# A hybrid decoder trunk: attention heads taken in pairs, with one output projection for both

## The chip, the cores and the metric

The kernel runs on one core of a Trainium2 chip. The metric is the device time of one execution in microseconds (us); lower is better. The core's engines have queues of their own and run beside each other: TensorE (PE, with its weight loads shown as PEld), VectorE (DVE), ScalarE (ACT), GpSimd (POOL) and SyncE (SP), which issues the DMAs. Matmuls write into PSUM, which has eight banks of 128 x 512 float32; DVE and ACT read them from there.

## The reference, cut to what matters

Two layers act on x of 1024 tokens by 1024 channels. Layer 0 mixes the tokens by a gated recurrence (HGRN2), layer 1 by latent attention (MLA) with 8 heads; behind each mixer stands a convolutional gated MLP. The change is in the attention:

```python
q = (_rmsnorm(c_q, q_a_norm) @ w_q_up).reshape(B, S, MLA_HEADS, MLA_QK_HEAD)
kv = (_rmsnorm(c_kv, kv_a_norm) @ w_kv_up).reshape(B, S, MLA_HEADS, MLA_NOPE + MLA_V_HEAD)
...
q = _rope_tail(_rmsnorm(q, q_norm), cos, sin)
k = _rope_tail(_rmsnorm(k, k_norm), cos, sin)
o = _causal_block_attention(q, k, v)
return o.reshape(B, S, MLA_HEADS * MLA_V_HEAD) @ w_out
...
x = x + y
h = _rmsnorm(x, norm_ffn[layer])
x = x + _conv_ffn(h, ffn_w_up[layer], ffn_conv_w[layer], ffn_conv_b[layer], ffn_w_down[layer])
```

The last product runs over all heads at once; the kernel sums it head by head.

## The kernel before, in words

The residual stream stays on the chip, transposed: two tiles `xt[0]` and `xt[1]`, one for each half of 512 tokens, each with 8 blocks of 128 channels. Float32 operands are split into a high and a low part (`split`, L124: ACT casts the high part at L126, DVE or POOL subtracts at L129), and each product is three matmuls: high by high, high by low, low by high (`acc3`, L142, matmuls at L145 to L147). Weights come by a DMA on SP's queue into one of two raw buffers (`fetch_w`, L86) and are split into one of three slots of the weight pool (`load_w`, L131); the output weight of a head has a slot of its own (tag "wo").

`mla` (L531) runs over the heads. For a head, `kproj` (L617) and `knorm` (L629) make its keys, `qproj` (L642) the queries of one half, `vproj` (L668) the values of two heads. `attend(hd, b, ...)` (L686) does two blocks of 128 queries, b from 0 to 3: scores at L701 into one of three banks, maxima on DVE (L706), exponentials on ACT (L716), scaling on POOL (L721), transposes at L730 with their split, the product with the values at L742 to L744 into a single bank, and a split of the result into the head's output tile, which holds one half. b = 0 and 1 fill the first half, 2 and 3 the second. Larger b have more keys and cost more.

`wout` (L748) is the output projection of one head and one half: for each of 8 channel blocks three matmuls of 512 columns into one of two banks ("mm", which all projections share), and `add_x` (L298) adds the bank to `xt` on DVE (L299). So head by head the residual is added to. The loop at L780 takes, for a head: attend 0, the second half's `wout` of the head before (`late`), the next head's `kproj`, attend 1, the next head's first `qproj`, attend 2, `wout` of the first half, the next head's `knorm`, attend 3, the next head's second `qproj`. Output tiles have two buffers. Keys alternate between the buffers "hh0" and "hh1", values lie in "hl1", the query latents in "hl0".

Behind the last head's attend 3 stands `first_half(1)` (L274): the norm of `xt[0]` for the MLP that follows (`normalize`, L261: sum of squares over the channels by `token_scale`, L200; scaling in place on DVE at L266; `xt` is also written to memory), and the split of its two halves of channels, LO and HI, into "hh0" and "hl0" (`operand`, L269). Then come the last `wout`, and in the MLP `second_half` (L278), for tokens 512 to 1023, and `open_strips` (L250): products of eight weight strips with the first half's two operands (L247), which need nothing of the second half. `hgrn` (L302) uses `first_half(0)` in the same way.

The program's order isn't written out by hand: a planner orders each engine's instructions ahead of time, by the order of the code and by when it expects them to be ready, and a later instruction may go ahead of an earlier one that isn't ready. On the chip each engine follows the order that is so fixed.

Of the kernel before, what the change touches and what calls it, by code (L numbers as in the profile page):

```python
# [10 lines left out]
F32R = mybir.dt.float32r  # L11
# [8 lines left out]
P = 128  # L20
D = 1024
S = 1024
HF = 512
KD = D // P
HEADS = 8
# [33 lines left out]
def trunk_kernel(ctx: ExitStack, tc: tile.TileContext, x, pos, par, gout, cst, msk, w_hin, w_hout,  # L59
# [6 lines left out]
    hpool = ctx.enter_context(tc.tile_pool(name="hpool", bufs=1))  # L66
# [4 lines left out]
    def ps_mm():  # L71
        return psg.tile([P, HF], F32, tag="mm", name="ps_mm")
# [8 lines left out]
    xt = [t.rearrange("p (k n) -> p k n", k=KD) for t in xflat]  # L81
# [49 lines left out]
    def load_w(src, tag="w", wp=None, bufs=3, eng=pool):  # L131
        lo_eng = dve if first else eng
        raw = first.pop(0) if first else fetch_w(src)
        hi = (wp or wpool).tile([P, 1024], F32R, tag=tag + "hi", name="whi", bufs=bufs)
        lo = (wp or wpool).tile([P, 1024], F32R, tag=tag + "lo", name="wlo", bufs=bufs)
        split(raw, hi, lo, lo_eng=lo_eng)
        return hi, lo

    def v3(ap, a):
        return ap.rearrange("p (a b) -> p a b", a=a)  # L140

    def acc3(ps, steps):  # L142
        n = len(steps)
        for i, (lh, ll, rh, rl) in enumerate(steps):
            pe.matmul(ps, lhsT=lh, rhs=rh, start=(i == 0), stop=False)  # L145
            pe.matmul(ps, lhsT=lh, rhs=rl, start=False, stop=False)  # L146
            pe.matmul(ps, lhsT=ll, rhs=rh, start=False, stop=(i == n - 1))  # L147
# [74 lines left out]
    def norm_x(hf, which, layer, spread=True, lo_eng=pool):  # L222
# [9 lines left out]
            return hh, hl, y, v  # L232
        return hh, hl, spread_scale(hf, y, lo_eng), y

    KH = KD // 2
    LO, HI = slice(0, KH), slice(KH, KD)
    OPENED = tuple(range(1, 17, 2))
# [5 lines left out]
    def product(p, a, b, first=True):  # L243
        for k in range(KH):
            ks = slice(k * P, (k + 1) * P)
# [23 lines left out]
    def operand(src, wp, tag):  # L269
        t = wp.tile([P, 2, KH, HF], F32R, tag=tag, name="bop", bufs=1)  # L270
        split(src, t[:, 0], t[:, 1], lo_eng=dve)
        return t

    def first_half(layer):  # L274
        normalize(0, layer)
        return [operand(xt[0][:, LO, :], hpool, "hh0"), operand(xt[0][:, HI, :], hpool, "hl0")]

    def second_half(layer, ep):  # L278
        normalize(1, layer)
# [251 lines left out]
    def mla(h):  # L531
        with ExitStack() as st:
            tp = st.enter_context(tc.tile_pool(name="m_t", bufs=2))
# [69 lines left out]

            wts = {}

            def weights(pr):
                wts["q", pr] = [v3(t, 2).rearrange("p k (h c) -> p k h c", h=2) for t in load_w(w_qup[pr])]
                wts["kv", pr] = [v3(t, 2).rearrange("p k (h c) -> p k h c", h=2) for t in load_w(w_kvup[pr])]

            def lora(w, c, hd, c0, hf):  # L610
                p = ps_mm()
# [5 lines left out]
            def kproj(hd):  # L617
                kgs, sqs = [], []
                for hf in range(2):
                    p = lora(wts["kv", hd // 2], ckv, hd, 0, hf)  # L620
                    sq = tpool.tile([P, HF], F32, tag="sq", name="ksq")
                    act.activation(out=sq, in_=p, func=AF.Square)
                    kg = tpool.tile([P, HF], F32, tag=f"rb{hf}", name="kg", bufs=1)
                    act.activation(out=kg, in_=p, func=AF.Identity, scale=pcol("kn", 0))
                    kgs.append(kg)
                    sqs.append([sq])
                return kgs, token_rstd(sqs, QK, krs.rearrange("p a b -> p (a b)"), tag="wo")

            def knorm(hd, kgs, y):  # L629
                kk = hpool.tile([P, 4, S], F32R, tag=f"hh{hd % 2}", name="kk")  # L630
                for hf in range(2):
                    sl = slice(hf * HF, (hf + 1) * HF)
                    rb = bcast(y[:, 4 * hf:4 * hf + 4], tag="wo")
                    kg = kgs[hf]
                    dve.tensor_tensor(out=kg, in0=kg, in1=rb, op=ALU.mult)
                    split(kg, kk[:, 0, sl], kk[:, 1, sl], lo_eng=dve)
                    kt = tpool.tile([P, HF], F32, tag="acc", name="kt", bufs=1)
                    dve.tensor_tensor(out=kt, in0=krot[:, hf, :], in1=rb, op=ALU.mult)
                    split(kt, kk[:, 2, sl], kk[:, 3, sl])
                return kk  # L640

            def qproj(hd, hf):  # L642
                qq = tp.tile([P, 3, HF], F32R, tag="q", name="qq")
                pn = lora(wts["q", hd // 2], cq, hd, 0, hf)
                pt = lora(wts["q", hd // 2], cq, hd, P, hf)
                sq = tpool.tile([P, HF], F32, tag="sq", name="qsq")
                act.activation(out=sq, in_=pn, func=AF.Square)
                sq2 = tpool.tile([P, HF], F32, tag="sq", name="qsq2")
                act.activation(out=sq2[0:64, :], in_=pt[0:64, :], func=AF.Square)
                pool.tensor_tensor(out=sq[0:64, :], in0=sq[0:64, :], in1=sq2[0:64, :], op=ALU.add)  # L650
                y = token_rstd([[sq]], QK, vq[:, hf, :], tag="wo")
                rq = tp.tile([P, 4], F32, tag="rq", name="rq")
                dve.tensor_scalar(out=rq, in0=y, scalar1=float(QK ** -0.5), scalar2=None, op0=ALU.mult)
                act.activation(out=qq[:, 0, :], in_=pn, func=AF.Identity, scale=pcol("qn", 0))
                dve.scalar_tensor_tensor(out=qq[:, 1, :], in0=pn, scalar=pcol("qn", 0),
                                         in1=qq[:, 0, :].bitcast(F32), op0=ALU.mult, op1=ALU.subtract)
                qt = tp.tile([P, 2, HF], F32, tag="qt", name="qt", bufs=1)
                for i in range(2):
                    rows = slice(64 * i, 64 * i + 64)
                    dve.scalar_tensor_tensor(out=qt[0:64, i, :], in0=pt[rows, :], scalar=pcol("qt", 0)[rows],  # L660
                                             in1=rope_t[rows, hf, :], op0=ALU.mult, op1=ALU.mult)
                rot = qt[0:64, 0, :]
                pool.tensor_tensor(out=rot, in0=rot, in1=qt[0:64, 1, :], op=ALU.add)
                act.copy(out=qq[0:64, 2, :], in_=rot)
                pool.tensor_tensor(out=qq[64:P, 2, :], in0=rot, in1=qq[0:64, 2, :].bitcast(F32), op=ALU.subtract)
                return qq, rq
# [78 lines left out]
                sl = slice((b % 2) * 2 * P, (b % 2 + 1) * 2 * P)  # L745
                split(po, oh[:, sl], ol[:, sl], lo_eng=dve)

            def wout(hf, wo, o):  # L748
                for d in range(KD):
                    p = ps_mm()  # L750
                    acc3(p, [(wo[0][:, d * P:(d + 1) * P], wo[1][:, d * P:(d + 1) * P], o[0], o[1])])
                    add_x(hf, d, p)

            def otile():
                return (tp.tile([P, HF], F32R, tag="oh", name="oh"), tp.tile([P, HF], F32R, tag="ol", name="ol"))

            wk = [load_w(w_min[2]), load_w(w_min[3])]
            wr = load_w(w_min[4])
# [6 lines left out]
            cq = clora(wq, cq_tile, "qa", 0, vq[:, 0, :], ps_s)  # L765
            h[1] = h[1]()
            clora(wk, ckv, "kva", 1, vc[:, 1, :])
            weights(0)
            rootc(0)
            ropek(wr, 1)  # L770
            rootc(1)
            kp = kproj(0)
            clora(wq, cq, "qa", 1, vq[:, 1, :], ps_s)
            kk = knorm(0, *kp)
            dve.tensor_scalar(out=vq, in0=vq, scalar1=EPS, scalar2=None, op0=ALU.mult)
            q0 = qproj(0, 0)
            vv = vproj(0)
            q1 = qproj(0, 1)
            late = None
            for hd in range(HEADS):  # L780
                more = hd + 1 < HEADS
                if more and hd % 2 == 1:
                    weights((hd + 1) // 2)
                o0 = otile()
                attend(hd, 0, kk, vv, *q0, *o0)
                if late:
                    wout(*late)
                wo = load_w(w_mout[hd], "wo", tp, 1)
                if more:
                    kp = kproj(hd + 1)  # L790
                attend(hd, 1, kk, vv, *q0, *o0)
                if more:
                    q0 = qproj(hd + 1, 0)
                o1 = otile()
                if not more:
                    wout(0, wo, o0)
                attend(hd, 2, kk, vv, *q1, *o1)
                if more:
                    wout(0, wo, o0)
                if more:  # L800
                    kk2 = knorm(hd + 1, *kp)
                attend(hd, 3, kk, vv, *q1, *o1)
                if not more:
                    h2 = first_half(1)
                late = (1, wo, o1)
                if more:
                    kk = kk2
                    q1 = qproj(hd + 1, 1)
                    if hd % 2 == 1:
                        vv = vproj((hd + 1) // 2)  # L810
            wout(*late)
            return h2

# [158 lines left out]
    h = [norm_x(0, "mix", 0, lo_eng=dve)]  # L972
    h = hgrn(0, h)
    h = ffn(0, h)
    h = mla(h)
# [77 lines left out]
```

## Time and profile before

| | us |
|---|---|
| median of 3 runs | 2605.51 |
| lowest, highest | 2604.63, 2606.7 |
| the profiled execution's own time | 2608.18 |
| its span, first to last instruction | 2606.4 |
| matmuls busy (share of the span) | 2474.9 (95%) |
| weight loads busy | 2043.3 (78%) |
| VectorE busy | 1795.3 (69%) |
| ScalarE busy | 1026.1 (39%) |
| GpSimd busy | 504.7 (19%) |

The profile shows one execution. Busy time is the union of an engine's instructions; matmuls are pipelined and overlap, so a busy PE isn't a PE at its peak. The granted clock of TensorE is 1.00 at full speed (2.4 GHz) and 0.5 at half. The attention's heads run from about 1440 to 1908 us of the span, the MLP of layer 1 follows. A row of the timeline has the start, the duration, the engine, the line, what is written and read, the count of merged instructions, and in brackets the engine's idle time before it and what ended it.

### The profile page before, as it was taken

The page shows a single profiled execution, that of the slowest core. Times are in us where ns is not written, and L with a number is a line of the kernel's source. Part 1 is how long each engine was busy: PE and PEld are TensorE (multiplying, and loading weights), DVE is VectorE, ACT ScalarE, POOL GpSimd, SP SyncE. Part 2 cuts the span into 40 slices and gives each one's busy share as a digit, 9 for nine tenths or more (in the row PEclk, how much of TensorE's full clock was granted, in tenths as well). Part 3 has the DMA queues.
Part 4 walks back from the last instruction along what each step waited for, and adds up shares of the span by engine and source line. Part 5 has one row for each costly group of instructions (what it writes and reads, how often), then busy time and mean ns, then how long its engine had stood idle before and what let it go on. Part 6 is the DMA issues. An engine that isn't in the chain of part 4 may idle for free.

```text
span 2606.4 us, 35442 instructions
## 1 busy us (share of the span) xinstructions
PE 2474.9 (95%) x13732; PEld 2043.3 (78%) x13732; DVE 1795.3 (69%) x3218; ACT 1026.1 (39%) x1697; POOL 504.7 (19%) x489
## 2 busy tenths in 40 slices
PE   7999999998889999999999999999879999999999
PEld 6888888887667778888888777777757777888887
DVE  7455565667778888774545887877878888875333
ACT  4322222232444444433433444444434444443322
POOL 4343333543000000000013444443400000000000
PEclk9999999999999999999999899999989999999999
DMA  3011100211323232264431000000033332226443
GB/s 145 34 41 41 33 33 25 74 59 56 117 97 117 105 107 90 95 226 154 137 115 57 9 17 17 17 25 9 33 123 123 110 109 101 97 88 223 153 169 119
DMA packets 67561, 228.21 MB, mean 88 GB/s; under 512 B 7616, under 2 KB 8000, under 8 KB 66240
## 3 DMA queue, kind: packets, MB, share of 16 engines
q1 hardware_dynamic: 67392, 225.94, 24.5%
q8 instruction: 108, 1.77, 0.3%
q14 instruction: 61, 0.50, 0.1%
HBM read 181.87 MB, written 44.04 MB: 87 GB/s over the span
## 4 chain that ended last, share of the span: by engine, by line
PE 77%; DVE 16%; ACT 3%; issue 2%; DMA 1%; POOL 0%; ACTq 0%; DVEq 0%; SPq 0%; POOLq 0%
PE ps_mm L247 18%; PE ps_up L247 8%; PE ps_up L946 7%; PE ps_mm L145 6%; PE ps_mm L147 6%; PE ps_mm L146 6%; PE ps_mm L946 5%; PE ps_wo L946 4%; PE ps_wo L247 3%; PE sc L388 2%; PE ps_misc L946 2%; DVE x L299 2%; PE sp L701 2%; PE ps_wo L145 1%; DMA wraw<-in_w_up_dram 1%
## 5 line engine op out<-in xcount | busy, mean ns | idle before, releaser
L126 ACT CAST whi<-wraw 128x1024 fp32r<-128x1024 f32 (+1 forms) x312 | 304.9, 991 | 564.1 <-PE ps_misc L946 240.9
L247 PE MATMUL ps_mm<-bop,whi 128*128 128x512 f32 x1536 | 485.3, 398 | 40.2 <-ACT bop L126 15.8
L129 DVE TENSOR_TENSOR wlo<-wraw,whi 128x1024 fp32r<-128x1024 f32 (+1 forms) x266 | 299.5, 1139 | 286.0 <-ACT whi L126 282.6
L247 PEld LDWEIGHTS ps_mm<-bop,whi 128*128 128x128 f32 x1536 | 290.3, 191 | 115.2 <-ACT bop L126 16.3
L247 PE MATMUL ps_mm<-bop,wlo 128*128 128x512 f32 x768 | 299.7, 395 | 0.9 <-DVE wlo L129 0.9
L866 DVE SCALAR_TENSOR_TENSOR x<-x,prm,x 128x1023 f32<-128x1023 f32 (+1 forms) x176 | 223.6, 1280 | 50.5 <-ACT x L863 49.5
L247 PE MATMUL ps_up<-bop,whi 128*128 128x512 f32 x704 | 221.6, 395 | 0.4 <-ACT whi L126 0.4
L247 PEld LDWEIGHTS ps_mm<-bop,wlo 128*128 128x128 f32 x768 | 146.2, 190 | 33.6 <-DVE wlo L129 1.4
L946 PE MATMUL ps_up<-ring,whi 128*128 128x512 f32 x528 | 159.8, 389 | 0.0
L247 PEld LDWEIGHTS ps_up<-bop,whi 128*128 128x128 f32 x704 | 132.0, 188 | 32.5 <-ACT whi L126 2.0
L129 POOL TENSOR_TENSOR wlo<-wraw,whi 128x1024 fp32r<-128x1024 f32 x46 | 113.2, 2463 | 219.3 <-ACT whi L126 219.3
L145 PE MATMUL ps_mm<-vgh,hh 128*128 128x256 f32 x512 | 145.1, 284 | 5.4 <-DVE q L355 5.4
L147 PE MATMUL ps_mm<-vgh,hl 128*128 128x256 f32 x512 | 145.0, 283 | 0.0
L146 PE MATMUL ps_mm<-vgl,hh 128*128 128x256 f32 x512 | 143.7, 281 | 0.0
L247 PE MATMUL ps_up<-bop,wlo 128*128 128x512 f32 x352 | 138.5, 394 | 0.0
L399 DVE TENSOR_TENSOR Q<-Q,tot 128x256 f32<-128x256 f32 x96 | 63.0, 656 | 103.7 <-PE sc L388 79.8
L863 ACT ACTIVATE x<-x,prm 128x1024 f32<-128x1024 f32 x88 | 109.5, 1244 | 62.0 <-DVE x L890 38.3
L701 PE MATMUL sp<-kk,qq 128*128 128x384 f32 (+4 forms) x480 | 112.1, 363 | 16.6 <-ACT pp L716 13.5
L849 DVE TENSOR_TENSOR wraw<-wraw 128x512 f32<-128x512 f32 x176 | 121.0, 688 | 2.1
L145 PE MATMUL ps_mm<-hh,whi 128*128 128x512 f32 x288 | 115.6, 402 | 2.5 <-DVE g L375 1.6
L401 POOL TENSOR_TENSOR K<-K,tot 128x256 f32<-128x256 f32 x96 | 78.4, 816 | 192.8 <-PE sc L388 124.1
L946 PEld LDWEIGHTS ps_up<-ring,whi 128*128 128x128 f32 x528 | 99.1, 188 | 20.6
(302 smaller groups left out, 5689.6 us busy)
## 6 DMA issues: line engine op xcount, KB each, us to landing
wraw<-in_w_up_dram SPq DMA_DIRECT2D x104, 512.0 KB, 3.7
wraw<-in_w_down_dram SPq DMA_DIRECT2D x88, 512.0 KB, 3.5
act_spill<-x SPq DMA_DIRECT2D x44, 512.0 KB, 2.6
araw<-act_spill SPq DMA_DIRECT2D x88, 256.0 KB, 3.6
wraw<-in_w_hin_dram SPq DMA_DIRECT2D x38, 512.0 KB, 3.5
x_spill<-x SPq DMA_DIRECT2D x4, 2048.0 KB, 6.7
open_spill<-part SPq DMA_DIRECT2D x32, 256.0 KB, 2.3
x<-open_spill SPq DMA_DIRECT2D x16, 512.0 KB, 3.2
```

The costliest lines, as they stand in the source:

```text
L126: act.copy(out=hi, in_=src)
L129: lo_eng.tensor_tensor(out=lo, in0=src, in1=hi.bitcast(F32), op=ALU.subtract)
L145: pe.matmul(ps, lhsT=lh, rhs=rh, start=(i == 0), stop=False)
L146: pe.matmul(ps, lhsT=lh, rhs=rl, start=False, stop=False)
L147: pe.matmul(ps, lhsT=ll, rhs=rh, start=False, stop=(i == n - 1))
L247: pe.matmul(p, lhsT=a[l][:, ks], rhs=b[:, r, k, :], start=first and k == 0 and n == 0, stop=k == KH - 1 and n == 2, skip_group_check=not f ...
L401: pool.tensor_tensor(out=Kv[:, :, 0, :], in0=Kv[:, :, 0, :], in1=tv[:, :, 1:2].broadcast_to([P, nb, m]), op=ALU.mult)
L701: pe.matmul(sp[:, 0:n], lhsT=qq[:, a, qs], rhs=kk[:, c, cl], start=(i == 0), stop=last)
L849: dve.tensor_tensor(out=o, in0=p, in1=q, op=op)
L863: act.activation(out=y, in_=u, func=AF.Identity, scale=cw(2, ff), bias=pcol("cb", layer * 44 + ff))
L866: dve.scalar_tensor_tensor(out=y[:, i:S], in0=u[:, 0:S - i], scalar=cw(2 - i, ff), in1=y[:, i:S], op0=ALU.mult, op1=ALU.add)
L946: pe.matmul(acc[d], lhsT=w[l][:, d * P:(d + 1) * P], rhs=a[:, r], start=j == 0 and n == 0, stop=j == NFF - 1 and n == 2)
```

## The change

Heads are taken in pairs a, b. The order is: attend 0 of a, `kproj` of b, the late `wout` of the pair before, attend 1 of a, `knorm` and first `qproj` of b, attends 0 and 1 of b with a's second `qproj` between them, `wout` of the first half for both heads, attends 2 and 3 of a with b's second `qproj` between, attends 2 and 3 of b with the next pair's keys and first queries between. `wout` takes both heads into the same bank, six matmuls for each of the 8 blocks, and adds once. The second output weight comes into one of the three slots of the weight pool. Query and key-value weights are loaded apart, at different places. In the last pair `first_half(1)` stands behind attend 3 of a. In `first_half` LO goes into "hl0" and HI into "hh0". The output tiles keep two buffers, now written out.

```diff
@@ -232,6 +232,7 @@
             return hh, hl, y, v
         return hh, hl, spread_scale(hf, y, lo_eng), y
 
+    OB = 2
     KH = KD // 2
     LO, HI = slice(0, KH), slice(KH, KD)
     OPENED = tuple(range(1, 17, 2))
@@ -273,7 +274,7 @@
 
     def first_half(layer):
         normalize(0, layer)
-        return [operand(xt[0][:, LO, :], hpool, "hh0"), operand(xt[0][:, HI, :], hpool, "hl0")]
+        return [operand(xt[0][:, LO, :], hpool, "hl0"), operand(xt[0][:, HI, :], hpool, "hh0")]
 
     def second_half(layer, ep):
         normalize(1, layer)
@@ -603,9 +604,9 @@
 
             wts = {}
 
-            def weights(pr):
-                wts["q", pr] = [v3(t, 2).rearrange("p k (h c) -> p k h c", h=2) for t in load_w(w_qup[pr])]
-                wts["kv", pr] = [v3(t, 2).rearrange("p k (h c) -> p k h c", h=2) for t in load_w(w_kvup[pr])]
+            def weights(kind, pr):
+                w = (w_qup if kind == "q" else w_kvup)[pr]
+                wts[kind, pr] = [v3(t, 2).rearrange("p k (h c) -> p k h c", h=2) for t in load_w(w)]
 
             def lora(w, c, hd, c0, hf):
                 p = ps_mm()
@@ -745,14 +746,16 @@
                 sl = slice((b % 2) * 2 * P, (b % 2 + 1) * 2 * P)
                 split(po, oh[:, sl], ol[:, sl], lo_eng=dve)
 
-            def wout(hf, wo, o):
+            def wout(hf, pair):
                 for d in range(KD):
+                    ds = slice(d * P, (d + 1) * P)
                     p = ps_mm()
-                    acc3(p, [(wo[0][:, d * P:(d + 1) * P], wo[1][:, d * P:(d + 1) * P], o[0], o[1])])
+                    acc3(p, [(wo[0][:, ds], wo[1][:, ds], o[0], o[1]) for wo, o in pair])
                     add_x(hf, d, p)
 
             def otile():
-                return (tp.tile([P, HF], F32R, tag="oh", name="oh"), tp.tile([P, HF], F32R, tag="ol", name="ol"))
+                return (tp.tile([P, HF], F32R, tag="oh", name="oh", bufs=OB),
+                        tp.tile([P, HF], F32R, tag="ol", name="ol", bufs=OB))
 
             wk = [load_w(w_min[2]), load_w(w_min[3])]
             wr = load_w(w_min[4])
@@ -765,7 +768,8 @@
             cq = clora(wq, cq_tile, "qa", 0, vq[:, 0, :], ps_s)
             h[1] = h[1]()
             clora(wk, ckv, "kva", 1, vc[:, 1, :])
-            weights(0)
+            weights("q", 0)
+            weights("kv", 0)
             rootc(0)
             ropek(wr, 1)
             rootc(1)
@@ -775,39 +779,44 @@
             dve.tensor_scalar(out=vq, in0=vq, scalar1=EPS, scalar2=None, op0=ALU.mult)
             q0 = qproj(0, 0)
             vv = vproj(0)
-            q1 = qproj(0, 1)
             late = None
-            for hd in range(HEADS):
-                more = hd + 1 < HEADS
-                if more and hd % 2 == 1:
-                    weights((hd + 1) // 2)
-                o0 = otile()
-                attend(hd, 0, kk, vv, *q0, *o0)
+            for a in range(0, HEADS, 2):
+                b, pr = a + 1, a // 2
+                more = b + 1 < HEADS
+                oa, ob = otile(), otile()
+                attend(a, 0, kk, vv, *q0, *oa)
+                kp = kproj(b)
                 if late:
                     wout(*late)
-                wo = load_w(w_mout[hd], "wo", tp, 1)
+                wos = [load_w(w_mout[a], "wo", tp, 1), load_w(w_mout[b])]
+                attend(a, 1, kk, vv, *q0, *oa)
+                kb = knorm(b, *kp)
+                q0 = qproj(b, 0)
                 if more:
-                    kp = kproj(hd + 1)
-                attend(hd, 1, kk, vv, *q0, *o0)
+                    weights("kv", pr + 1)
+                attend(b, 0, kb, vv, *q0, *ob)
+                q1 = qproj(a, 1)
+                attend(b, 1, kb, vv, *q0, *ob)
+                wout(0, list(zip(wos, (oa, ob))))
+                oa, ob = otile(), otile()
+                attend(a, 2, kk, vv, *q1, *oa)
+                q0 = qproj(b, 1)
                 if more:
-                    q0 = qproj(hd + 1, 0)
-                o1 = otile()
-                if not more:
-                    wout(0, wo, o0)
-                attend(hd, 2, kk, vv, *q1, *o1)
+                    weights("q", pr + 1)
+                attend(a, 3, kk, vv, *q1, *oa)
                 if more:
-                    wout(0, wo, o0)
+                    kp = kproj(b + 1)
+                else:
+                    h2 = first_half(1)
+                attend(b, 2, kb, vv, *q0, *ob)
                 if more:
-                    kk2 = knorm(hd + 1, *kp)
-                attend(hd, 3, kk, vv, *q1, *o1)
-                if not more:
-                    h2 = first_half(1)
-                late = (1, wo, o1)
+                    kk = knorm(b + 1, *kp)
+                    q1 = qproj(b + 1, 0)
+                attend(b, 3, kb, vv, *q0, *ob)
+                late = (1, list(zip(wos, (oa, ob))))
                 if more:
-                    kk = kk2
-                    q1 = qproj(hd + 1, 1)
-                    if hd % 2 == 1:
-                        vv = vproj((hd + 1) // 2)
+                    vv = vproj(pr + 1)
+                    q0 = q1
             wout(*late)
             return h2
```

## Rows read from the trace of the kernel before

**Rows 1.** The page, part 1: busy us, share of the span, instructions.

```profile
PE 2474.9 (95%) x13732; PEld 2043.3 (78%) x13732; DVE 1795.3 (69%) x3218; ACT 1026.1 (39%) x1697; POOL 504.7 (19%) x489
```

**Rows 2.** Busy time by stretch: start:end, length, then each engine's busy us.

```profile
core 0: us, PE busy (x) PEld busy (x) DVE busy (x) ACT busy (x) POOL busy (x), PEclk, DMA share, GB/s
...
1552.00:1669.00 117.00, 106.43 (x620) 86.55 (x619) 96.16 (x253) 54.55 (x120) 49.32 (x57) 1.00 0.06 19
...
1876.00:1892.00 16.00, 11.77 (x66) 9.64 (x66) 14.03 (x30) 10.58 (x24) 7.45 (x8) 1.00 0.20 81
1892.00:1908.50 16.50, 14.55 (x69) 10.83 (x69) 10.28 (x27) 4.41 (x8) 0.57 (x3) 0.90 0.20 82
1908.50:1924.00 15.50, 2.40 (x5) 1.09 (x6) 14.19 (x18) 7.24 (x8) 4.44 (x3) 0.58 0.32 135
```

**Rows 3.** Timeline of PE in an output projection, around 1666 us.

```profile
1665.99 0.50 PE L145 MATMUL ps_mm<-oh,whi 128*128 128x512 f32 x1 [0.43 <-DVE x L299]
...
1666.56 0.39 PE L147 MATMUL ps_mm<-oh,wlo 128*128 128x512 f32 x1
1666.79 0.62 PE L701 MATMUL sp<-kk,qq 128*128 128x256 f32 x4
```

**Rows 4.** Waits, 1440 to 1925 us: total us, times, longest us.

```profile
PEld ps_mm L145 <- DVE x L299: 22.4, 40, 1.3
PEld sp L701 <- ACT pp L716: 20.0, 23, 1.8
...
PE ps_mm L145 <- DVE x L299: 7.5, 14, 0.9
```

**Rows 5.** Groups by line, 1440 to 1925 us: count, busy us, mean ns, idle before.

```profile
L299 DVE TENSOR_TENSOR x<-x,ps_mm 128x512 f32<-128x512 f32 x128 | 86.0, 680 | 4.5 <-PE ps_mm L147 3.6
...
L129 POOL TENSOR_TENSOR wlo<-wraw,whi 128x1024 fp32r<-128x1024 f32 x12 | 28.9, 2407 | 45.3 <-ACT whi L126 45.3
...
L126 ACT CAST whi<-wraw 128x1024 fp32r<-128x1024 f32 x15 | 15.8, 1051 | 36.7 <-PE ps_mm L146 32.0 <-DMA wraw<-in_w_qup_dram 2.5 <-DMA wraw<-in_w_up_dram 2.0
```

**Rows 6.** The chain that ended last, 1440 to 1925 us, shares by line.

```profile
by line: PE sp L701 8.5%; PE ps_mm L145 8.1%; DVE x L299 8.1%; PE ps_mm L147 6.1%; PE ps_mm L146 6.1%; issue 4.2%; DVE mx L706 4.1%; DVE tl L129 3.1%; PE ps_misc L165 2.9%; DVE st_z L155 2.9%; PE ps_wo L730 2.6%; DVE kk L129 2.6%; ACT pp L7
```

**Rows 7.** Timeline of PE at the end of the attention.

```profile
1892.21 0.88 PE L730 MATMUL ps_wo<-ident,pp 128*128 128x128 f32 x6 [3.45 <-POOL pp L721]
...
1910.04 1.00 PE L197 MATMUL ps_misc<-dg,ones_r 128*128 128x512 f32 x2 [1.55 <-DVE dg L189]
1921.45 1.22 PE L247 MATMUL ps_mm<-bop,whi 128*128 128x512 f32 x2 [10.41 <-ACT bop L126]
1923.78 0.80 PE L247 MATMUL ps_mm<-bop,whi 128*128 128x512 f32 x1 [1.11 <-DVE bop L129]
...
1925.66 0.63 PE L247 MATMUL ps_mm<-bop,wlo 128*128 128x512 f32 x1
1926.08 1.05 PE L247 MATMUL ps_mm<-bop,whi 128*128 128x512 f32 x2
...
1928.20 0.39 PE L247 MATMUL ps_mm<-bop,wlo 128*128 128x512 f32 x1
```

**Rows 8.** Timeline of DVE at the end of the attention.

```profile
1911.70 8.43 DVE L266 SCALAR_TENSOR_TENSOR x<-x,prm,rb 128x512 f32<-128x512 f32 x8 [1.21 <-ACT rb L219]
...
1921.44 4.49 DVE L129 TENSOR_TENSOR bop<-x,bop 128x2048 fp32r<-128x2048 f32 x2
```

**Rows 9.** Timeline of PE: the first matmul of a query projection.

```profile
1850.47 0.50 PE L145 MATMUL ps_mm<-cq,whi 128*128 128x512 f32 x1 [0.74 <-DVE x L299]
```

**Rows 10.** Timeline of POOL: the last operation of the same projection.

```profile
1862.70 1.27 POOL L665 TENSOR_TENSOR qq<-qt,qq 64x512 fp32r<-64x512 f32 x1 [0.73 <-ACT qq L664]
```

**Rows 11.** The line of the scores: idle time before it, us and times.

```profile
  ACT kk L126: 6.8, 9
```

**Rows 12.** Waits of SP's queue, 1440 to 1925 us.

```profile
SPq L88 <- POOL wlo L129: 271.0, 7, 56.1
```

**Rows 13.** DMA issues, 1440 to 1925 us: count, size, median us to landing.

```profile
wraw<-in_w_qup_dram SPq DMA_DIRECT2D x2, 512.0 KB, 3.4
```

## The prediction, made before the changed kernel was run

> **What bounds the kernel now.** The page comes first: over the whole span TensorE's matmuls are busy 95%, VectorE 69% [rows 1]. The change touches one stage, so the table by stretch is next [rows 2]. In a steady pair of heads (1552 to 1669 us) 117 us hold 106 us of matmul busy time, 87 us of weight loads and 96 us of DVE. Nothing else is near a limit: ACT has 55, POOL 49. So two engines share the stage and neither is full. That PE looks fuller than it is can be read in the timeline [rows 3]: a 512-column matmul shows 0.39 or 0.40 us, yet the next starts 0.23 us later, and after a gap the first shows 0.50. About 0.16 us of each gap is thus painted busy.
>
> What PE waits for in the stage, from 1440 to 1925 us, is in the table of waits [rows 4]: the weight load of an output projection waits 40 times, 22.4 us, for the residual add at L299 (the matmuls themselves show 7.5 us of it), and those of scores wait 20.0 us for the exponential that frees a bank. The adds are the costliest DVE group of the stage, 128 of 0.68 us, 86.0 us [rows 5], and the chain through the stage passes through them for 8.1% of 485 us, 39 us [rows 6]. The reason is in the shape of the loop at L749: three matmuls of 0.23 us fill a bank in 0.69 us, one add empties it in 0.68, two banks are shared with every other projection, and DVE has softmax work between two adds.
>
> The end of the stage is a second place [rows 2, 7, 8]. From 1908.5 to 1924 us PE is busy 2.4 us of 15.5 at a granted clock of 0.58: it waits 1.55 us for the diagonal of the norm, 10.41 us for the cast of the first operand, 1.11 us for its low part, 13.1 us in all, while DVE does eight scalings (8.43 us) and two splits (4.49 us). Before that stands one wait of 3.45 us for POOL's last softmax scaling.
>
> **The change, part by part.**
>
> *Half the adds.* 8 heads x 2 halves x 8 = 128 adds become 4 pairs x 2 x 8 = 64, of 0.68 us [rows 5]: 43.5 us of DVE less; the matmuls stay 384. Six matmuls (1.38 us) now fill a bank against one add, so the add is done before the bank is wanted again. The worth lies between PE's own shown wait, 7.5 us [rows 4], and the whole DVE time, 43.5 us. I take half of what the chain has of these adds, 39 / 2 = 20 us, since half of the adds go; the 22.4 us that the weight loads wait is close to it. What is late next is the softmax chain: scores behind the exponential.
>
> *The next layer's first half is worked out before the last two attends* instead of behind the last one. Its DVE work stays, 8.43 + 4.49 = 12.9 us [rows 8], but is moved ahead of work that PE needs. From 1876 to 1908.5 us DVE is busy 14.03 + 10.28 of 32.5 us [rows 2], so 8.2 us fit beside what is there and 4.7 us come in the way. Gone are the 13.1 us of PE waits and the 3.45 us one, which products of the opened strips can fill: 13.1 + 3.45 - 4.7 = 11.9, I take 12 us. Ends: nothing, if all 12.9 us of DVE work gets in the way of 13.1 us, and 16.6 us. The row nearest is the window itself, where DVE had room, hence near the upper end. A second half follows as before behind the last projection.
>
> The profile shows that such a gap costs twice: behind the 10.41 us the clock is at 1.2 GHz, matmuls show 0.63 us and start 0.42 apart, about 12 of them until 1928.20 us, 12 x 0.19 = 2.3 us [rows 7]. The Trainium skill, "TensorE: Matmul & The Clock Gate", section "Why this matters for your kernels", says that idle stretches between bursts of matmuls put the clock back to half. By the trace that holds here, and by it the sum would be some 2 us better; I leave it out because a new wait could bring this back.
>
> *Operands in swapped buffers.* LO goes where the query latents were and HI where head 6's keys were; both are free by the last two attends. The recurrent layer uses the same function, but its two buffers come free together. I cost it at nothing: the last-but-one attend covers it, and without that cover it is one wait for a split, 4.49 / 2 = 2.2 us [rows 8].
>
> *Moved projections and weights.* The query and key projections of the second head stand right before its first attend; before, the next head's first query half stood two attends ahead of its use. From its first matmul (1850.47) to its last operand (POOL's subtraction, 1862.70 + 1.27) one such projection took 13.5 us [rows 9, 10]. Scores queue behind it in PE's order. Once a pair that is exposed between 0 and 13.5 us; a small gain isn't excluded either, as scores wait 6.8 us for keys now, 9 times by 0.75 us [rows 11]. Those waits are the nearest row: I take 1 us a pair, 4 us in all. The loads stay 4 + 4 + 8, with the same cast and subtraction each; on SP's queue they keep their number, and SP itself waits for POOL to free the raw buffers (seven times, up to 56.1 us [rows 12]), so it is ahead of need; a landing takes 3.4 us [rows 13]. The second output weight now holds one of three weight slots for a pair, so the next query weights can come only when the old ones are done: landing, cast 1.05 and subtraction 2.41 are 6.9 us [rows 5, 13], covered by two attends; without that cover the bound is 6.9 x 3 = 21 us. I take nothing.
>
> *Two buffers for four outputs.* The first attend of a pair can't write its output until the late projection of the pair before has read its own, 48 matmuls x 0.23 = 11 us. PE does that work anyway, so I take nothing; the upper end is 11 us at each of three boundaries.
>
> Sum: -20 - 12 + 4 = -28 us on the profiled execution's 2608.2 us, 2580. That execution is 2.7 us above the median of the runs, 2605.5, so 2577 us. Some 5 us (0.2%) is what a measurement of this kernel tells from no change.
>
> **The rivals.**
>
> *The second head starves (slower).* Each pair's query projection is emitted just ahead of its use; if nothing ready is left to fill PE, all 13.5 us show: 4 x 13.5 = 54 us against 32 gained, 22 us slower, 2627. It decides from 8 us a pair (32 / 4). For it: the chain of small DVE steps and POOL's operations of 1.27 us in a projection [rows 10]. Against: 11 us of late projection are at hand to fill.
>
> *Work comes apart.* Two output projections in one run keep PE for 11 us with only 8 x 0.68 = 5.4 us of DVE beside it; twice a pair DVE then idles 5.6 us, 11 us a pair, as much as the 16 adds saved (10.9 us). The loop gains nothing, only the end does: 2605.5 - 12 = 2593. The three matmuls a bank of today let scores in between [rows 3]; nothing of the trace shows six. The Trainium skill, "Perfetto Trace Analysis", section "Optimization Strategy", says that regimes with different limits gain from being interleaved; this change sorts them instead, and a row for its size is missing.
>
> *DVE is the bound after all.* Then all 43.5 us count: 2605.5 - 43.5 - 12 + 4 = 2554. For it: DVE 82% busy in a steady pair; against: PE is nearly as full [rows 2], and softmax chains cross both.
>
> That the adds do not halve is excluded by the loop itself; that two buffers make the halves serial is the 11 us above.
>
> **How the numbers follow.** Forecast 0.52, apart 0.20, starved 0.16, DVE-bound 0.12. Faster by over 0.2%: 0.49 of the forecast, 0.12, and 0.15 of the case that comes apart, 0.76. Within: 0.03 and 0.05, 0.08. Slower: 0.16. The range goes down to the DVE-bound case, 2553, and up through the case that comes apart to a little above no change, 2612; left out are most of the starved case and the rest of the DVE-bound one.
>
> **What would show it.** L299 has 64 adds in the stage; PE's waits for it fall under 5 us; a pair takes 110 to 113 us; the gap before L247 is gone and no clock of 0.58 stands there. Wrong would be: waits of scores for query or key operands over 8 us a pair (starved), or DVE idle rising by as much as the adds free (apart).

## The result and the profile after

The changed kernel takes **2648.4 us** (median of 4 runs, 2645.8 to 2649.6) against 2606.1 before: ratio 1.0156, interval 1.0143 to 1.0168. It is slower by 42 us, where 2577 us was forecast, with a range of 2553 to 2612.

Part 1 of the page, after:

```profile
PE 2495.8 (94%) x13732; PEld 2062.0 (78%) x13732; DVE 1763.7 (67%) x3154; ACT 1026.1 (39%) x1697; POOL 509.9 (19%) x489
```

Against [rows 1], DVE lost the 64 instructions that the change takes out, and 32 us. The adds alone fell by 43 us (128 to 64), so DVE's other work shows some 11 us more, which no run explains. PE has the same 13,732 matmuls, and they took 21 us longer. The time is lost in the loop over the pairs. The table by stretch shows it, cut at each pair's first score, with the columns of [rows 2]; the last stretch ends with the last product with the values. First before:

```profile
1439.00:1547.00 108.00, 99.60 (x547) 83.90 (x545) 91.38 (x246) 52.62 (x116) 48.70 (x53) 0.91 0.05 15
1547.00:1663.00 116.00, 106.27 (x620) 86.57 (x618) 95.16 (x254) 53.78 (x120) 49.56 (x56) 1.00 0.06 19
1663.00:1780.00 117.00, 106.98 (x619) 87.94 (x620) 95.45 (x255) 54.51 (x122) 47.19 (x56) 0.99 0.04 14
1780.00:1900.00 120.00, 105.86 (x616) 88.45 (x614) 97.43 (x236) 56.91 (x124) 44.66 (x55) 0.97 0.11 40
```

Then after:

```profile
1437.00:1558.00 121.00, 105.52 (x555) 88.44 (x555) 84.62 (x224) 52.03 (x116) 46.68 (x52) 0.86 0.03 9
1558.00:1684.00 126.00, 110.97 (x618) 91.56 (x618) 89.07 (x238) 54.20 (x121) 50.34 (x56) 0.95 0.05 18
1684.00:1811.00 127.00, 112.57 (x619) 93.09 (x618) 88.95 (x239) 54.50 (x121) 50.19 (x56) 0.93 0.05 17
1811.00:1949.00 138.00, 111.84 (x604) 92.65 (x602) 102.04 (x251) 60.54 (x127) 49.45 (x55) 0.89 0.08 31
```

The four pairs grew from 461 to 512 us. What follows them shrank from 706 to 697 (the span less 1900, and less 1949), and they start 2 us earlier: 51 - 10 - 2 = 39 us between the two profiled spans, 2606.4 and 2645.5. Look at the two middle pairs, which hold the same work in both (1239 and 1237 matmuls on record). They took 253 us for 233. PE was busy 223.5 for 213.3 at a granted clock of 0.94 for 1.00, and idle 29.5 for 19.8. So half of the loss is PE standing still, and half is the same matmuls shown busy for longer, which fits the lower clock (a part of it may be the time that is painted busy at each gap). DVE's idle time went from 21 to 37.5 us a pair: more than the adds set free.

What PE waits for in these two pairs is in the table of waits (total us, times, longest), before from 1547 to 1780 us:

```profile
PE sp L701 <- ACT pp L716: 7.3, 11, 1.5
PE ps_mm L145 <- DVE x L299: 4.1, 8, 0.8
```

and after, from 1558 to 1811 us:

```profile
PE ps_misc L743 <- ACT vv L682: 5.0, 2, 2.5
PE ps_wo L731 <- POOL pp L722: 4.7, 2, 2.3
PE ps_mm L145 <- DVE qt L661: 3.5, 4, 1.5
PE sp L702 <- ACT pp L717: 3.3, 4, 1.3
PE sp L702 <- POOL qq L666: 3.2, 2, 1.6
PE ps_misc L744 <- DVE tl L129: 3.1, 4, 1.2
```

The adds are gone from the list, and the exponential's wait has halved. In their place stand the values `vv` (5.0 us; products with the values did not wait for them before), POOL's scaling `pp` (4.7 us against 0.7), and the small operations of the query projections: `qt` and `qq` in front of a shared bank or of a score. In the table of the whole stage, 1440 to 1975 us, these lines matter below:

```profile
PE ps_misc L744 <- DVE tl L129: 14.3, 11, 4.9
...
PE sp L702 <- POOL qq L666: 3.5, 3, 1.6
PE sp L702 <- ACT kk L126: 3.2, 4, 1.4
```

The wait for `tl` (the split of the transposed weights, 4.2 us before) is the longest of all, but 10.9 of its 14.3 us stand in the last pair, into which the first half's DVE work was moved, and 3.1 in the two middle ones, for 1.9 before. The group of the adds' line, 1440 to 1965 us:

```profile
L300 DVE TENSOR_TENSOR x<-x,ps_mm x64: 673/687/690, 1503.7 to 1960.1; 128x512 f32<-128x512 f32 x64
its engine sat idle before it (us, times) until:
  PE ps_mm L147: 19.4, 39
who waited for it (us, times):
...
  PE ps_mm L145: 0.3, 1
```

Now DVE waits for PE in front of an add (19.4 us; 3.6 before), and PE for an add only 0.3 us. The timeline of PE at the start of a pair's first joint projection gives a first suspect for the waits elsewhere:

```profile
1607.99 0.50 PE L145 MATMUL ps_mm<-oh,whi 128*128 128x512 f32 x1 [0.91 <-DVE qq L656]
...
1610.55 0.50 PE L702 MATMUL sp<-kk,qq 128*128 128x256 f32 x2 [1.59 <-POOL qq L666]
...
1613.46 0.77 PE L145 MATMUL ps_mm<-oh,whi 128*128 128x512 f32 x1 [1.50 <-DVE qt L661]
1614.02 0.63 PE L146 MATMUL ps_mm<-ol,whi 128*128 128x512 f32 x1
...
1628.58 0.62 PE L145 MATMUL ps_mm<-oh,whi 128*128 128x512 f32 x2
```

Three matmuls of the first head opened a bank at 1607.99, three more the other at 1613.46; the next such matmul came at 1628.58, when the second head's output existed. In between PE did little but the attends' own work, with gaps, and some matmuls of 512 columns took 0.63 us for 0.39. The next two runs try whether these open banks are the cause.

### The profile page after: what moved, and what is told of

It reads as the page before. It is cut to its first block, busy times and chain, and to the rows that moved or that the text cites. A ratio compares the mean times of both kernels' runs of the same rounds, so it can differ in the third digit from the quotient of the medians.

```text
span 2645.5 us, 35402 instructions
## 1 busy us (share of the span) xinstructions
PE 2495.8 (94%) x13732; PEld 2062.0 (78%) x13732; DVE 1763.7 (67%) x3154; ACT 1026.1 (39%) x1697; POOL 509.9 (19%) x489
## 4 chain that ended last, share of the span: by engine, by line
PE 80%; DVE 13%; ACT 3%; issue 2%; DMA 1%; POOL 1%; SPq 0%; ACTq 0%; DVEq 0%; POOLq 0%
PE ps_mm L248 17%; PE ps_up L248 8%; PE ps_up L955 7%; PE ps_mm L145 6%; PE ps_mm L147 6%; PE ps_mm L146 6%; PE ps_mm L955 4%; PE ps_wo L955 4%; PE sp L702 3%; PE ps_wo L248 3%; PE ps_misc L955 2%; PE sc L389 2%; PE ps_misc L165 1%; PE ps_wo L145 1%; PE ps_wo L147 1%
## 5 line engine op out<-in xcount | busy, mean ns | idle before, releaser
L129 POOL TENSOR_TENSOR wlo<-wraw,whi 128x1024 fp32r<-128x1024 f32 x46 | 113.4, 2469 | 213.3 <-ACT whi L126 213.2
L702 PE MATMUL sp<-kk,qq 128*128 128x384 f32 (+4 forms) x480 | 121.4, 391 | 19.7 <-ACT pp L717 11.2
L147 PE MATMUL ps_mm<-hh,wlo 128*128 128x512 f32 x288 | 114.9, 399 | 0.0
```

The costliest lines, as they stand in the source:

```text
L129: lo_eng.tensor_tensor(out=lo, in0=src, in1=hi.bitcast(F32), op=ALU.subtract)
L702: pe.matmul(sp[:, 0:n], lhsT=qq[:, a, qs], rhs=kk[:, c, cl], start=(i == 0), stop=last)
```

## Experiments

Ratios are to the kernel before, measured together with the run; the 95% interval stands beside each.

**Is it the two banks opened early?** Two kernels: the second head's matmuls go first in the joint projection, so that a bank opens only when all is ready (e1); or each head has its own banks and adds, at the same places (e2).

```
e1, at both places:
-  list(zip(wos, (oa, ob)))
+  list(zip(wos, (oa, ob)))[::-1]
e2, in wout:
-  acc3(p, [(wo[0][:, ds], wo[1][:, ds], o[0], o[1]) for wo, o in pair]); add_x(hf, d, p)
+  for wo, o in pair: (8 strips) acc3(p, [(wo[0][:, ds], wo[1][:, ds], o[0], o[1])]); add_x(hf, d, p)
```

> Held banks: the three matmuls of the first head open both shared banks as soon as that head's output is there and keep them until the second head's output comes, so no other projection gets a bank. With the second head's three matmuls first, a bank is opened only when both outputs are there: each joint projection is one run of 11 to 15 us in place of 36 to 50 us, and the time falls by 40 us or more, to 2570 to 2610 us. Starved projections (the order of the query and key projections is the cause): nothing that they wait for changes, 2640 to 2650 us.

Measured: 2659.1 us, 1.0193 (1.0179 to 1.0207), above both ranges.

> The order of the change, but each head's output projection with banks and adds of its own (128 adds again). Held banks: no bank stays open across an attend, so most of the loss goes although 43 us of adds come back: 2590 to 2625 us. Starved projections: the order is the same, and the adds come on top: 2645 to 2665 us.

Measured: 2657.7 us, 1.0196 (1.0182 to 1.0210). The theory that the banks held by the output projection cost the time falls: without them the kernel is some 10 us slower still. By e2 the joint projection with its halved adds is worth 2657.7 - 2648.4 = 9 us in the new order, and all else in the change costs 50.

**The swapped operands alone**, in the kernel before.

```
-  return [operand(xt[0][:, LO, :], hpool, "hh0"), operand(xt[0][:, HI, :], hpool, "hl0")]
+  return [operand(xt[0][:, LO, :], hpool, "hl0"), operand(xt[0][:, HI, :], hpool, "hh0")]
```

> The kernel before with the two buffers of the first operand swapped and nothing else. Both theories: within 0.2% of the kernel before, 2601 to 2611 us.

Measured: 2607.5 us, 1.0000 (0.9991 to 1.0009). Nothing, as forecast.

**Is it the place of the output projections?** e2 with its four projections of a pair spread between four attends, about as the kernel before has them.

```
 attend(b, 0, ...)
+wout(0, [(wos[0], oa)])
 ...
 attend(a, 2, ...)
+wout(0, [(wos[1], last)])
 ...
 attend(b, 2, ...)
+wout(1, [(wos[0], oa)])
 ...
+late = (1, [(wos[1], ob)])
```

> Pair order as in the change, heads projected apart (128 adds), and the four projections of a pair spread out: the first head's behind attend 0 and attend 2 of the second head, the second head's behind attend 2 of the first and in the next pair. Work comes apart (long stretches of attends with no projection to fill PE): most of the loss goes, 2600 to 2625 us. Starved (query and key projections stand just ahead of their use): it stays, 2645 to 2660 us.

Measured: 2637.0 us, 1.0118 (1.0104 to 1.0132). Spreading gives back 20 us of e2's 50. Both theories miss: the place counts, but it isn't all. The table by stretch of the changed kernel, in a middle pair, is cut at the late joint projection, the stretch that holds the other one, and the rest, in which no output projection runs:

```profile
1583.00:1597.00 14.00, 13.89 (x66) 11.12 (x66) 11.53 (x30) 4.75 (x8) 5.80 (x4) 1.00 0.12 39
1597.00:1645.00 48.00, 42.29 (x222) 33.98 (x221) 34.16 (x90) 18.94 (x45) 20.80 (x24) 0.93 0.07 23
1645.00:1710.00 65.00, 55.81 (x330) 47.62 (x329) 43.12 (x117) 30.73 (x68) 23.43 (x28) 0.92 0.03 9
```

PE stands still for 0.1 us of the 14, 5.7 of the 48 and 9.2 of the 65: the late projection runs as one block, and the gaps lie where there is less or nothing of the kind to fill them.

e4 lifts a second thing together with the place. In the order of the change both output tiles are still to be read by the late projection when the next pair's first attend wants to write its own. After, PE's timeline has the last product of that attend, and ACT's the cast of its result:

```profile
1575.64 0.41 PE L745 MATMUL ps_misc<-th,vv 128*128 128x256 f32 x1
1596.83 0.36 ACT L126 CAST oh<-ps_misc 128x256 fp32r<-128x256 f32 x1
```

The cast comes right behind the late projection's last matmul (1596.24), and until then the single bank for products with the values is taken; so it is at all three boundaries, some 20 us each. In e4, as before, the cast comes 0.3 us behind the product. No run parts the place of the projections from this wait, so the 20 us are the price of both.

**Does the second head starve?** In the changed kernel the key norm and the second head's first query projection go one attend earlier.

```
+kb = knorm(b, *kp)
+qb = qproj(b, 0)
 attend(a, 1, ...)
-kb = knorm(b, *kp)
-q0 = qproj(b, 0)
+q0 = qb
```

> The changed kernel with the second head's key norm and first query projection one attend earlier, ahead of attend 1 of the first head. Starved: 7 us a pair or more come back, 2595 to 2620 us. Work comes apart: within 10 us of the changed kernel, 2636 to 2655 us.

Measured: 2644.7 us, 1.0145 (1.0131 to 1.0159). Only about 4 us better (3 by the ratios), and the two intervals overlap: the starved rival is not the cause of more than that.

**The first half early, alone**, in the kernel before (with the swapped operands it needs).

```
+h2 = first_half(1)
 attend(hd, 2, ...)
 ...
 attend(hd, 3, ...)
-h2 = first_half(1)
```

> The kernel before, head by head, with nothing of the pairs but the end: the next layer's first half ahead of the last two attends, and the two operand buffers swapped. In the changed kernel the stretch from the last value product to the end of the span is 10 us shorter than before. If that is this edit's own, 2592 to 2600 us; if it came with the pairs, 2603 to 2610 us.

Measured: 2610.2 us, 1.0013 (1.0004 to 1.0022): 3.5 us slower, no gain. The table by stretch of this run, with the columns and two of the stretches of [rows 2]:

```profile
1892.00:1908.50 16.50, 9.16 (x36) 7.94 (x36) 12.35 (x28) 5.65 (x7) 0.41 (x2) 0.50 0.12 49
1908.50:1924.00 15.50, 12.04 (x49) 9.36 (x48) 9.00 (x13) 4.99 (x9) 3.03 (x5) 0.71 0.00 0
```

The hole was not filled but moved: PE, busy 14.55 us in the first stretch before, now has 9.16 there at half clock. Its waits, 1876 to 1930 us, name who is late:

```profile
PE ps_wo L730 <- POOL pp L721: 4.5, 1, 4.5
PE ps_misc L197 <- DVE dg L189: 3.5, 1, 3.5
PE ps_misc L743 <- DVE tl L129: 2.8, 1, 2.8
PE ps_misc L742 <- DVE ol L129: 2.5, 1, 2.5
```

These are 13.3 us: the last softmax behind the first half's DVE work (5.39 us of scalings stand ahead of this `tl`, 4.49 us of splits ahead of this `ol`), and the norm's own diagonal. Before, the 13.1 us at the end and the 3.45 us of POOL stood there, 16.5 us. The waits shrank by 3 us, and the time didn't, with the granted clock at 0.50 for 0.90 in the first of the two stretches and 0.71 for 0.58 in the second.

**Half the adds, alone**, in the kernel before: the adds of every second head are left out.

```
-  add_x(hf, d, p)
+  if add:            # add = (hd % 2 == 1)
+      add_x(hf, d, p)
```

> The kernel before with the residual adds of every even head left out (64 of 128, their products are computed and dropped), order unchanged: the worth of the halved adds by itself. As forecast, 16 to 24 us: 2582 to 2592 us. Hidden behind PE and the softmax chain: 2600 to 2610 us. VectorE as the bound: about 2563 us.

Measured: 2594.8 us, 0.9951 (0.9938 to 0.9963): 12 us, not 20. In the two middle pairs DVE's busy time fell from 95 to 87 and 88 us:

```profile
1547.00:1663.00 116.00, 108.75 (x635) 91.41 (x635) 86.76 (x244) 55.10 (x122) 51.06 (x57) 0.97 0.06 19
1663.00:1780.00 117.00, 108.92 (x651) 91.34 (x650) 88.33 (x249) 56.24 (x125) 49.77 (x57) 1.00 0.04 14
```

These are stretches at the times of the kernel before. They hold 47 more matmuls (635 and 651 for 620 and 619), which at 217.7 / 1286 = 0.17 us of busy time each is 8 us of work come forward; a trace can lack a few records, so this is a rough share of the 12. DVE has 16 us less work in the two, and as the stretches are of fixed length, so much more idle time.

**Are the banks held by the values?** The changed kernel with two value buffers: only one of the two value parts is kept, which makes room for the second buffer (e8). The same edit in the kernel before is the control (e9).

```
-  vv = hpool.tile([P, 8, 2, 256], F32R, tag="hl1", name="vv")
+  if pr == 0: vbig.append(hpool.tile([P, 2, 8, 256], F32R, tag="hl1", name="vv"))
+  vv = vbig[0][:, pr % 2]
```

> The changed kernel with two buffers for the values of a pair in the room of one (only the low part is kept, so the output differs; the count of operations is the same). Held by the values: the first two blocks of the next pair's values fill both shared banks and keep them some 30 us, until the last value product of the pair frees the single buffer; without that wait 20 us or more come back, 2628 us or less. Work comes apart: within 10 us of the changed kernel, 2638 to 2655 us.

Measured: 2637.0 us, 1.0117 (1.0102 to 1.0132).

> The same edit in the kernel before, as a control. Both theories: 2600 to 2612 us, as the values there come behind the query projection and wait for nothing long.

Measured: 2607.9 us, 1.0005 (0.9995 to 1.0014). So the edit does nothing by itself, and in the changed kernel it gives 11 us, between the two ranges. What it takes away is seen in the group of the projections' first matmul line, 1535 to 1600 us (count, duration in ns, first and last start). Before:

```profile
L145 PE MATMUL ps_mm<-whi,ckv x16: 276/279/363, 1561.7 to 1571.5; 128*128 128x256 f32 x16
```

After:

```profile
L145 PE MATMUL ps_mm<-whi,ckv x16: 279/283/415, 1540.8 to 1577.8; 128*128 128x256 f32 x16
```

e8:

```profile
L145 PE MATMUL ps_mm<-whi,ckv x16: 278/280/388, 1542.6 to 1554.4; 128*128 128x256 f32 x16
```

The next pair's value projection took 10 us before, 37 after and 12 in e8. The timeline of ACT, after, shows what it waited for:

```profile
1570.04 0.37 ACT L126 CAST oh<-ps_misc 128x256 fp32r<-128x256 f32 x1 [1.19 <-PE ps_misc L745]
1570.31 0.85 ACT L682 ACTIVATE vv<-ps_mm,rc 128x256 fp32r<-128x256 f32 x2
```

The values may be written only when the pair's last product with the old values is done; the cast of its result is at 1570.04, and the first write at 1570.31. From about 1544 until then the two shared banks hold finished values, and no query, key or output projection can pass.

**Bunching**, in the kernel before: both output projections of a head follow each other behind the next head's first attend.

```
-if late:
-    wout(*late)
+for w in late or ():
+    wout(*w)
 ...
-if more: wout(0, wo, o0)
 ...
-late = (1, wo, o1)
+late = [(0, wo, o0)] * more + [(1, wo, o1)]
```

> The kernel before, head by head with 128 adds, but both output projections of a head stand together, behind attend 0 of the next head (the last head as before). Work comes apart: attends 2 and 3 lose the projection that filled PE, 20 us or more slower, 2626 to 2650 us. Held by the values, or starved: 2602 to 2615 us.

Measured: 2634.2 us, 1.0102 (1.0085 to 1.0119): 27 us slower, with the same counts of instructions. The table by stretch, a middle pair:

```profile
1552.00:1675.00 123.00, 108.63 (x606) 87.54 (x605) 94.05 (x247) 54.14 (x119) 47.75 (x55) 0.97 0.05 18
```

and the value projection, in the same view as above:

```profile
L145 PE MATMUL ps_mm<-whi,ckv x16: 279/280/582, 1549.4 to 1580.2; 128*128 128x256 f32 x16
```

In the 123 us are fewer matmuls (606 for 620 in [rows 2]) at a clock of 0.97. Here too the value projection came forward by 12 us and stood open for 31: with no output projection at hand, it is the work that is ready. And the output tiles are held, too. Two lines of the waits, 1440 to 1950 us:

```profile
ACT oh L126 <- PE ps_mm L147: 20.8, 3, 6.9
...
PE ps_mm L145 <- DVE qt L660: 16.1, 8, 2.9
```

ACT stands three times before the cast of an output until the bunched projection has read the tile (the kernel before shows no such wait). What grew most among PE's waits is not a link of the softmax chain but the shared bank that a query projection holds (`qt` 16.1 us and `qq` 5.1, neither in the list of PE's waits before); the softmax links change by little or fall (`tl` 5.4 for 4.2, the exponential 14.2 for 13.5, `pp` 1.0 for 5.3). So the 27 us are the price of bunching with all that it brings, not of bare softmax chains alone.

**Both together**: e4's places and e8's buffers (the edits are above).

> The spread-out pairs of the fourth run with two buffers for the values (low part only, output differs). Held by the values: 15 us or more below that run, 2605 to 2622 us. Work comes apart: what is left there has another cause, 2627 to 2642 us.

Measured: 2621.6 us, 1.0056 (1.0041 to 1.0071): 15 us less than e4. The table by stretch, cut at its own pairs:

```profile
1437.00:1558.00 121.00, 104.75 (x553) 86.35 (x553) 90.67 (x243) 52.09 (x115) 46.23 (x52) 0.90 0.03 9
1558.00:1676.00 118.00, 108.62 (x622) 89.85 (x621) 97.13 (x254) 55.71 (x123) 51.85 (x57) 0.97 0.05 19
1676.00:1794.00 118.00, 108.09 (x614) 89.63 (x613) 96.61 (x252) 54.29 (x120) 50.49 (x57) 0.96 0.06 19
1794.00:1924.00 130.00, 110.46 (x624) 92.12 (x622) 108.12 (x266) 60.74 (x127) 45.93 (x56) 0.89 0.09 33
```

The middle pairs are back within 2 us of before. What is left stands in the first pair (121 for 108) and the last (130 for 120); 14 us of these 23 come back in the tail (2616 - 1924 = 692 us for 706).

**Is the rest starvation?** e11 with e5's edit.

> The eleventh run (spread projections, two value buffers) with the second head's key norm and first query projection one attend earlier. Starved: what that run still loses stands in the first pair, between attend 1 of the first head and attend 0 of the second (about 12 us of PE time from 1463 to 1489 us); 4 to 12 us come back, 2609 to 2618 us. Another cause: 2619 to 2626 us.

Measured: 2656.5 us, 1.0191 (1.0177 to 1.0205): 35 us worse, which neither theory expected. From the waits of PE, 1440 to 1975 us:

```profile
PE ps_misc L748 <- DVE tl L129: 21.9, 13, 4.9
```

The wait for `tl`, a link of the softmax chain, rose from 13.9 us in e11 to 21.9. That the projection's many small operations stand in front of that chain on DVE and ACT would fit; it was not tried apart, and 8 us are far from 35: the cause stays open.

**Can ACT and POOL carry the adds?** In the kernel before, every second add becomes a copy on ACT and an add on POOL.

```
+if d % 2 == 0:
+    act.copy(out=t, in_=p)
+    pool.tensor_tensor(out=xt[hf][:, d, :], in0=xt[hf][:, d, :], in1=t, op=ALU.add)
+else:
     add_x(hf, d, p)
```

> The kernel before, order unchanged, with every second residual add of the attention made by ACT (copy out of the bank) and POOL (add) in place of VectorE. If the time that the seventh run gained is VectorE's to give: 8 us or more faster, 2590 to 2599 us. If ACT and POOL, which both stand in the softmax chain, take it back: 2602 to 2620 us.

Measured: 2611.8 us, 1.0017 (1.0008 to 1.0025): 5 us slower. The waits, 1440 to 1925 us, all engines:

```profile
ACT wsq L754 <- PE ps_mm L147: 54.3, 37, 5.1
...
PE sp L701 <- ACT pp L716: 18.3, 23, 1.2
```

ACT now stands waiting for output projections (54.3 us) with the exponentials behind it, and PE's wait for the exponential rises from 13.5 to 18.3 us. DVE has as many adds less as by the change; what that is worth, 12 us by e7, the two other engines took back, and 5 more.

No kernel that does all the work beat the one before.

## Why the prediction was wrong, point by point

- **Halved adds, -20.** Right in sign, too large: 12 us alone (e7), 9 in the new order, with the banks held (e2 against the changed kernel). The step that failed is reading half of the chain's 39 us as worth. The shown waits of PE, 7.5 us, were the nearer end. The forecast's own test (64 adds, waits under 5 us) came true, and told nothing of the time.
- **First half early, -12.** Alone +3.5 (e6). Of its bounds, nothing at all was the nearer. The step that failed is "8.2 us fit beside what is there": DVE's idle time between softmax links is no room for blocks of 5.39 and 4.49 us, since the link that comes ready in one waits. In the changed kernel the gap of 10.41 us is gone, and the tail is 10 us shorter, but the last pair is 11 us longer than its neighbour.
- **Moved projections, +4.** Not contradicted: e5 gives back 3 to 4 us in the changed kernel, though within the intervals. But in e12 the same move costs 35, so this term depends on what stands around it.
- **Swapped operands, 0.** Right (e3). The weight slots were not tried by themselves; no wait for weights is among PE's long ones.
- **Output projections in one run.** This is the step that failed most. The forecast's sum has no term for it; the nearest is "PE does that work anyway", said of the late projection. The rival "work comes apart" named the place, and its sign (DVE idle up by as much as the adds free) came true. But it looked for DVE's idle time beside the joint projection, where the late one has 2.5 us of it in 14; 22 us in 65 lie where no projection runs (under e4). And its price was only the adds' gain lost: 2593. The runs: bunching in the head order of before costs 27 us (e10), and spreading the projections gives back 20 of 50 (e2 to e4), the wait for the output tiles included. That an output projection is the work with which PE covers the chains of small DVE, ACT and POOL steps beside it, of softmax and query projection alike, fits the stretches under e4; no run shows it by itself.
- **What no term or rival named:** with nothing else ready, the next pair's value projection comes forward, fills both shared banks, and waits there for the old values to be read for the last time. With a second buffer 11 us are gone (e8) or 15 (e11), without effect before (e9).
- **Two buffers for four outputs, 0.** The wait that this term names is there, some 20 us at each of three boundaries (under e4). What it costs was not tried alone and stays open; it is within the 20 us of e4.

The sum by runs: e2's 50 us are 20 for the place and the output tiles (e4), 15 for the values (e11) and some 15 that stay open (e11); the joint projection gives 9 back, which makes 41 or 42. Of the open part, the profile says only where it is: in the first pair and the last, where the first half's DVE work stands.

The starved rival gave the nearest time, 2627, but by luck, not by its mechanism: scores wait 3.5 us for queries and 3.2 for keys in the whole stage, where it asked for over 8 a pair. The Trainium skill, "Perfetto Trace Analysis", section "Optimization Strategy", which favours interleaving regimes with different limits, is borne out by e2 and e4; the size that the prediction missed is there 20 us, and in e10, where more than the order changes, 1.0%.

## What to carry to other kernels

Before moving a block of PE work because "PE does it anyway", list what it lies beside: if its neighbours are chains of short steps over several engines, it may be their cover, and its place can be worth more than the instructions saved: 20 us against 9 here, output tiles included. Ask which buffers stay taken for longer in the new order. Ask also which ready work will move into the hole, and whether it takes a shared bank that it can't give back before some old buffer is free. An engine's idle time summed over a stretch is not room for one long block ahead of a chain.

## What the runs showed of the hardware

Small gaps cost twice, too. The longest idle stretch of PE in the middle pairs after is 2.48 us, for the 10.41 us of [rows 7], yet the granted clock there is 0.93 to 0.95 for 0.99 to 1.00, and 1237 matmuls show 223.5 us of PE where 1239 show 213.3. The timeline of the result has such a place: behind idle stretches of 0.91, 1.59 and 1.50 us, matmuls of 512 columns show 0.63 us, as at 1.2 GHz in [rows 7], for 0.39. The Trainium skill, "TensorE: Matmul & The Clock Gate", section "Why this matters for your kernels", has idle stretches put the clock back; the trace agrees. By an estimate from these rows, up to 10 of the 20 us that the two pairs lost are the clock's.
